# Three unused tiles that shift operands in SBUF by 64 and by 96 bytes

## The chip, the cores and the metric

One core of a Trainium2 chip runs one step of a small diffusion trunk. The metric is the device time of one execution in microseconds. Three runs of the kernel before took 601.01, 600.64 and 601.30 us; the median is 601.01.

## The reference

One layer reads 1024 latent tokens and 128 context tokens of width 1024 (nine tiles of 128 tokens, the last of them context), in float32. Cut to what matters:

```python
mod = silu(cond) @ w_ada + b_ada                 # shift, scale, gate
h = rmsnorm(x, norm_g) * (1 + scale) + shift
u, v, g_a, c_q, c_kv, k_rope, g_b = split(h @ w_in)      # 2496 columns
a_out = chunk_mlp(u, v, w_s, b_s, g_v) * silu(g_a)       # 128x128 position mixing
q = (rmsnorm(c_q, q_norm_g) @ w_uq)                      # 4 heads, 128 + 64 rope
ckv = rmsnorm(c_kv, kv_norm_g); k, val = ckv @ w_ukv
attn = softmax(q k^T / sqrt(192)) @ val   # latent rows see latent and 256 cached keys
y = concat([a_out, attn * silu(g_b)]) @ w_o
out = rmsnorm(x + gate * y, final_g)      # also returned: new_ckv, new_krope
```

## The kernel before, in words

Each float32 operand of a product is split into a high part, rounded to the type that TensorE reads in one pass, and a low part, the remainder. A product is then three matmuls: high by high, high by low, low by high. In `T.matmul(out, a, b)` the operand `a` is the stationary one (loaded 128 columns at a time) and `b` the moving one, whose columns (256, 384, 448 or 512) stream past it. In a row of the profile the moving operand stands first behind the arrow: `o<-ph,vh` moves ph against vh.

The stages follow one another on TensorE:

- head (0 to some 60 us): x and the modulation weights `ada` are loaded (L313, L475), the modulation is computed, x is normalised, transposed and split into `area`, and the v part of the projection starts (L443 to L448, L371 to L373);
- projection (60 to 235 us): the rest of `h @ w_in` on sums of blocks, in runs of matmuls of 384 columns (L928 and L949) that move `area`, the block sums in `w1t`, or the small tiles `t4h` (one) and `t4l` (two), against the weights `w` and `s`;
- q and kv (235 to 310 us): 448-column products (L1371 to L1373), then the parts of q and the keys (L158 to L160);
- attention (310 to 500 us): scores (L1500 to L1504, L1526 to L1533) move the keys `kch`, `kcl`, `krh`, `krl` against q, which lies in `area`; ScalarE writes the exponentials `e` (L1481), GpSimd scales them (L1486), TensorE transposes them (L1609), ScalarE and VectorE split the result into `ph` and `pl`, and the value products (L1633 to L1635) move these against `vh` and `vl`;
- output projection (500 to 592 us): again on block sums, 512-column products (L1970 to L1972) that move parts of `w_o` in `area`, `kch` and its like, `vht`, `vlt`, or in the tail tiles `t` (t4), `t1a`, `t1c`, `t1h`, `t1l`; the stationary blocks are slices of `area` and the rings B and C.

The order of the work on each engine is written by planners in the kernel (`Plan.run`, `merged`, `later`) from costs and due times that stand in the code. None of them looks at an address. TensorE's queue runs in that order, SP issues most loads in program order.

SBUF is handed out from two ends. A pool opened with `side="left"` stands above the left pools opened before it, one with `side="right"` below the right pools opened before it. `ht` (the three `area` tiles) is the first left pool. All later left pools (`w1`, `va`, `vb`, `kv`, `tp`, `wo` and others) stand on top of it, so they move with it. The right pools hold, among others, the identity `ident`, the gates' product `mixB`, the q parts (`cqh`, `wfh`), and, one after the other at the same place, the pool `at` (e, ph, pl) and the pool `ep` of the output stage (tail tiles, gate0, fg, xr, own). Both `at` and `ep` grow from the same lower end upward.

Of the kernel before, what the change touches and what calls it, by code (L numbers as in the profile page):

```python
# [9 lines left out]
F32 = mybir.dt.float32  # L10
# [8 lines left out]
P = 128  # L19
# [75 lines left out]
def tile_hymba_step(ctx: ExitStack, tc: tile.TileContext, I, O):  # L95
# [3 lines left out]
    def opened(name, bufs=1, space=None, side=None):  # L99
        kw = dict(name=name, bufs=bufs, reuse_waits="tile")  # L100
        if space is not None:
            kw["space"] = space
        if side is not None:
            kw["side"] = side
        cm = tc.tile_pool(**kw)
        return cm, cm.__enter__()
# [4 lines left out]
    def lo_of(lo, src, hi):  # L111
        V.tensor_tensor(lo, src, f32(hi), op=ALU.subtract)  # L112
# [54 lines left out]
    def later(dt, fn):  # L167
        waiting.append((now[0] + dt, fn))
        waiting.sort(key=lambda w: w[0])
# [27 lines left out]
    def need(*keys):  # L197

        at_ = now[0]
        while waiting and not made.issuperset(keys):  # L200
            due, fn = waiting.pop(0)
            now[0] = due
            fn()
        now[0] = at_
        assert made.issuperset(keys), keys
# [52 lines left out]


    c_ht, ht = opened("ht", side="left")  # L260
    c_w1, w1 = opened("w1", side="left")
    c_va, va = opened("va", side="left")
    c_vb, vb = opened("vb", side="left")
# [1180 lines left out]
    c_at, ap_ = opened("at", side="right")  # L1444
# [53 lines left out]
    def logits(ps, qs, sl):  # L1498
        qh_, ql_, qr_ = qs
        T.matmul(ps, qh_, kch[:, sl], start=True, stop=False)  # L1500
        T.matmul(ps, qh_, kcl[:, sl], start=False, stop=False)
        T.matmul(ps, ql_, kch[:, sl], start=False, stop=False)
        T.matmul(ps, qr_, krh[:, sl], start=False, stop=False)
        T.matmul(ps, qr_, krl[:, sl], start=False, stop=True)  # L1504
# [229 lines left out]
    def own_steps():  # L1734

        sl, ks = slice(2 * P, 3 * P), slice(NS * P, NT * P)
        four = lambda ap: ap.rearrange("p (h c) -> p h c", h=4)
        cell = {}

        def score():  # L1740
            ps = cell["s"] = pso.tile([P, 512], F32, tag="o", name="s8")
            for h in range(4):
                logits(ps[:, h * P : (h + 1) * P], (qnh[2][:, h, sl], qnl[2][:, h, sl], qr[2][:, 1, h, sl]), ks)
            later(1.3, shift)

        def shift():
            e = cell["e"] = ap_.tile([P, 1280], F32, tag="e", name="e8", bufs=6)
            m = sm.tile([P, 4], F32, tag="m8", name="m8", bufs=1)
            nb = cell["nb"] = sm.tile([P, 4], F32, tag="nb8", name="nb8", bufs=1)
            su = cell["su"] = sm.tile([P, 4], F32, tag="su8", name="su8", bufs=1)  # L1750
            V.tensor_reduce(m, four(cell["s"]), axis=AX.X, op=ALU.max)
            V.tensor_scalar(nb, m, nscl[:, NS : NS + 1], None, op0=ALU.mult)
            for h in range(4):
                c_ = slice(h * P, (h + 1) * P)
                S.activation(e[:, c_], cell["s"][:, c_], AF.Exp, bias=nb[:, h : h + 1], scale=scl[:, NS : NS + 1], accum_out=su[:, h : h + 1])
            later(3.7, divide)

        def divide():
            rs = sm.tile([P, 4], F32, tag="rs8", name="rs8", bufs=1)
            V.reciprocal(rs, cell["su"])  # L1760
            e4 = four(cell["e"][:, :512])
            G.tensor_tensor(e4, e4, rs.unsqueeze(2).broadcast_to([P, 4, P]), op=ALU.mult)
            made.add("e8")

        def tr():
            need("e8")
            ps = pst.tile([P, 512], F32, tag="t", name="pT8")
            for h in range(4):
                T.transpose(ps[:, h * P : (h + 1) * P], cell["e"][:, h * P : (h + 1) * P], ident)
            cell["ph"] = ap_.tile([P, 512], F32R, tag="ph", name="ph8", bufs=4)  # L1770
            cell["pl"] = ap_.tile([P, 512], F32R, tag="pl", name="pl8", bufs=4)
            later(0.5, lambda: S.copy(cell["ph"], ps))

            def low():
                lo_of(cell["pl"], ps, cell["ph"])
                made.add("p8")

            later(1.15, low)

        def av():  # L1780
            need("p8")
            o = cell["o"] = pso.tile([P, 512], F32, tag="o", name="o8")
            T.matmul(o, vh[:, NS, :], cell["ph"], start=True, stop=False)
            T.matmul(o, vh[:, NS, :], cell["pl"], start=False, stop=False)
            T.matmul(o, vl[:, NS, :], cell["ph"], start=False, stop=True)
            cell["os"] = cell["e"][:, 512:1024]

            def out():
                S.copy(cell["os"], o)
                made.add("o8")  # L1790

            later(0.8, out)

        def up():
            need("o8")
            ps = pso.tile([P, 512], F32, tag="o", name="at8")
            for h in range(4):
                T.matmul(ps[:, h * P : (h + 1) * P], wuv[:, h, :], cell["os"][:, h * P : (h + 1) * P], start=True, stop=True)
            d = mixB[:, :, NS * P : NT * P]
            later(1.0, lambda: V.tensor_tensor(d, d, four(ps), op=ALU.mult))  # L1800

        return [(1.1, score), (0.45, tr), (0.65, av), (0.85, up)]

    heads = [(t, h) for t in range(NS) for h in range(4)]
# [267 lines left out]
    def place(name, w, dt=F32R):  # L2072
        return ep.tile([P, w], dt, tag=name, name=name)
# [2 lines left out]
    t1h, t1a = place("t1h", 512), place("t1a", 2048)  # L2076
    gate0, fg = place("gate0", 1024, F32), place("fg", 1024, F32)
    t1c, t1l = place("t1c", 1024), place("t1l", 512)
    t4 += [kv.tile([P, 1024], F32R, tag=n, name=f"{n}t") for n in ("vh", "vl")]
    th[1, 3], tl[1, 3] = t1h, t1l  # L2080
    gate, ssq = {}, {}
# [115 lines left out]
    for q in range(3, len(queue)):  # L2197
        n, name, _ = queue[q]
# [279 lines left out]
```

## Time and profile before

| | before |
|---|---|
| median of three runs | 601.01 us |
| the profiled execution's own time | 600.68 us |
| its span, first to last instruction | 598.9 us |
| mean granted TensorE clock | 0.997 |
| TensorE matmuls, busy | 588.7 us, 3653 |
| weight loads, busy | 527.0 us, 3653 |
| VectorE, ScalarE, GpSimd busy | 428.7, 329.7, 213.5 us |
| DMA | 67.33 MB, mean 112 GB/s |

The weight load of the next matmul runs beside the matmul of now. A matmul's time in a row is the time from its start to the end of its drain, and the next one starts before that, so rows overlap. In the timeline the columns are start (us from the span's start), duration (us, of all merged instructions of the row), engine, line, operation, tiles, shape and count. In the table by stretches they are the stretch, its length, busy us with counts in brackets for TensorE, weight loads, VectorE, ScalarE and GpSimd, the granted clock, the share of the DMA engines and GB/s.

### The profile page before, as it was taken

What the parts mean: (1) busy time and instruction counts of PE and PEld (TensorE: products, weight loads), DVE (VectorE), ACT (ScalarE), POOL (GpSimd) and SP (SyncE); (2) the same over time, 40 slices, a digit from 0 to 9 for tenths busy, and PEclk for the clock granted to TensorE, in tenths of its full rate; (3) what the DMA queues carried; (4) which work ended last, traced back from release to release, by engine and by line L of the source; (5) the groups of instructions that cost most, each with busy time, mean ns of one, the idle gap of its engine ahead of it and who ended that gap; (6) DMA issues with size and microseconds to landing.
All of it is one profiled execution on the core that took longest, in us unless ns stands there. A gap on an engine that the chain in (4) does not pass through costs nothing.

```text
span 598.9 us, 10175 instructions
## 1 busy us (share of the span) xinstructions
PE 588.7 (98%) x3653; PEld 527.0 (88%) x3653; DVE 428.7 (72%) x946; ACT 329.7 (55%) x771; POOL 213.5 (36%) x251
## 2 busy tenths in 40 slices
PE   8999999999999999999999999999999999999995
PEld 7578889999999999999998888888888898888884
DVE  3676888967647467476678677778788876477885
ACT  6665886434323245455567556655756462457543
POOL 2562103200000000343264345454543547269834
PEclk9999999999999999999999999999999999999998
DMA  8991002051050134100002033434242019951444
GB/s 314 366 378 74 1 4 68 1 210 71 7 207 26 45 96 138 42 1 0 2 8 71 0 106 111 156 123 142 85 144 90 1 71 307 359 178 39 140 153 161
DMA packets 31059, 67.33 MB, mean 112 GB/s; under 512 B 3344, under 2 KB 17440, under 8 KB 29984
## 3 DMA queue, kind: packets, MB, share of 16 engines
q1 hardware_dynamic: 27792, 55.93, 26.7%
q0 software_dynamic: 2352, 8.39, 4.1%
q10 hardware_dynamic: 864, 2.36, 1.2%
q8 instruction: 29, 0.48, 0.3%
q14 instruction: 22, 0.18, 0.1%
HBM read 53.45 MB, written 13.21 MB: 111 GB/s over the span
## 4 chain that ended last, share of the span: by engine, by line
PE 92%; DMA 3%; POOL 2%; DVE 1%; ACT 1%; issue 0%; SPq 0%; POOLq 0%; ACTq 0%
PE p L928 15%; PE tp L949 7%; PE pT L1609 5%; PE o L1633 3%; PE o L1635 3%; PE o L1634 3%; PE zacc L1372 2%; PE zacc L1371 2%; PE zacc L1373 2%; PE S L1970 2%; PE S L1971 2%; PE S L1972 2%; DMA ada<-in_ada_ss 2%; PE s L1526 2%; PE s L1529 2%; PE s L1528 2%
## 5 line engine op out<-in xcount | busy, mean ns | idle before, releaser
L1486 POOL TENSOR_SCALAR e<-e,rs 128x1280 f32<-128x1280 f32 x32 | 47.0, 1470 | 96.8 <-DVE rs L1485 64.7
L112 DVE TENSOR_TENSOR pl<-pT,ph 128x512 fp32r<-128x512 f32 x81 | 55.5, 686 | 32.8 <-ACT ph L1613 32.6
L1481 ACT ACTIVATE e<-s,nb,scl 128x256 f32<-128x256 f32 x64 | 56.9, 891 | 38.8 <-DVE nb L1469 26.2
L1613 ACT CAST ph<-pT 128x512 fp32r<-128x512 f32 x80 | 47.2, 590 | 40.6 <-PE pT L1609 40.3
L1219 POOL TENSOR_TENSOR kr<-z,rope 128x64 f32<-128x64 f32 x8 | 2.6, 326 | 154.6 <-ACT z L1228 154.6
L949 PE MATMUL tp<-area,w 128*128 128x384 f32 x288 | 52.5, 337 | 0.0
L1633 PE MATMUL o<-ph,vh 128*128 128x256 f32 x160 | 50.7, 317 | 0.0
L949 PEld LDWEIGHTS tp<-area,w 128*128 128x128 f32 x288 | 50.4, 188 | 0.0
L1609 PE MATMUL pT<-ident,e 128*128 128x128 f32 x320 | 47.9, 272 | 0.0
L1609 PEld LDWEIGHTS pT<-ident,e 128*128 128x128 f32 x320 | 38.9, 140 | 7.2
L1635 PE MATMUL o<-ph,vl 128*128 128x256 f32 x160 | 45.1, 282 | 0.0
L1634 PE MATMUL o<-pl,vh 128*128 128x256 f32 x160 | 44.8, 280 | 0.0
L1463 DVE TENSOR_REDUCE m<-s 128x1 f32<-128x1024 f32 x32 | 38.9, 1216 | 2.6 <-PE s L1504 2.5
L1633 PEld LDWEIGHTS o<-ph,vh 128*128 128x128 f32 x160 | 30.2, 188 | 4.7 <-ACT os L1643 2.9
L1634 PEld LDWEIGHTS o<-pl,vh 128*128 128x128 f32 x160 | 30.3, 189 | 0.4
L1635 PEld LDWEIGHTS o<-ph,vl 128*128 128x128 f32 x160 | 30.1, 188 | 0.0
L928 PE MATMUL p<-area,w 128*128 128x384 f32 x144 | 27.6, 337 | 0.0
L928 PE MATMUL p<-area,s 128*128 128x384 f32 x144 | 27.3, 337 | 0.0
L1371 PE MATMUL zacc<-w1t,area 128*128 128x448 f32 x72 | 27.0, 375 | 0.0
L928 PE MATMUL p<-w1t,s 128*128 128x384 f32 x144 | 26.6, 339 | 0.0
L1372 PE MATMUL zacc<-w1t,area 128*128 128x448 f32 x72 | 26.3, 366 | 0.0
L1373 PE MATMUL zacc<-w1t,area 128*128 128x448 f32 x72 | 26.3, 365 | 0.0
(703 smaller groups left out, 1767.8 us busy)
## 6 DMA issues: line engine op xcount, KB each, us to landing
ada<-in_ada_ss SPq DMA_DIRECT2D x16, 512.0 KB, 8.6
w2r<-in_w_t SPq DMA_DIRECT2D x12, 512.0 KB, 5.3
x<-in_x SPq DMA_DIRECT2D x9, 512.0 KB, 5.6
adag<-in_ada_g SPq DMA_DIRECT2D x4, 1024.0 KB
traw<-in_w_o SPq DMA_DIRECT2D x16, 256.0 KB, 3.0
tdram<-thi SPq DMA_DIRECT2D x32, 128.0 KB, 1.8
tdram<-traw SPq DMA_DIRECT2D x32, 128.0 KB, 1.8
wor<-in_w_o SPq DMA_DIRECT2D x8, 512.0 KB, 3.8
```

Source lines behind the costliest of these rows:

```text
L112: V.tensor_tensor(lo, src, f32(hi), op=ALU.subtract)
L928: T.matmul(banks[key], a_, b_, start=k == 0 and m == 0, stop=k == 3 and m == len(passes) - 1)
L949: T.matmul(tps[c, 2][:, :GW], w_[c][:, k, :], x_[k, 2], start=k == 0 and m == 0, stop=k == NK - 1 and m == 2)
L1371: T.matmul(ps[:, :448], a, wqh[k], start=k == 0, stop=False)
L1463: V.tensor_reduce(m[:, 0:1], lat_, axis=AX.X, op=ALU.max)
L1481: S.activation(e[:, sl], src, AF.Exp, bias=nb, scale=scl[:, t : t + 1], accum_out=su[:, i : i + 1])
L1486: G.tensor_scalar(e, e, rs, 0.0, op0=ALU.mult, op1=ALU.add)
L1609: T.transpose(ps[:, w : w + P], es[t, h][:, c * P : (c + 1) * P], ident)
L1613: later(0.5, lambda: S.copy(ph[:, :w], ps[:, :w]))
L1633: T.matmul(o, vh[:, kt, :], ph[:, sl], start=c == 0, stop=False)
L1634: T.matmul(o, vh[:, kt, :], pl[:, sl], start=False, stop=False)
L1635: T.matmul(o, vl[:, kt, :], ph[:, sl], start=False, stop=c == n - 1)
```

## The change

Three tiles are added that nothing writes or reads. One of 16 float32 (64 bytes in each partition) is the first tile behind `area`'s pool opening, ahead of the `area` tiles, so every left pool stands 64 bytes higher. One of 24 float32 (96 bytes) is asked for in the pool `at` in the first unit of the attention; there `ph` and `pl` keep their places and the `e` tiles lie 96 bytes lower. One of 96 bytes in `ep` does the same for the tail tiles and for gate0 and fg, while `xr` and `own` stay. All instructions, their order on the five queues and what they wait for are the same in the two kernels.

```diff
     c_ht, ht = opened("ht", side="left")
+    ht.tile([P, 16], F32, tag="edge", name="edge2")
     c_w1, w1 = opened("w1", side="left")
     c_va, va = opened("va", side="left")
...
                 T.transpose(ps[:, h * P : (h + 1) * P], cell["e"][:, h * P : (h + 1) * P], ident)
+            ap_.tile([P, 24], F32, tag="edge", name="edge0")
             cell["ph"] = ap_.tile([P, 512], F32R, tag="ph", name="ph8", bufs=4)
...
     t1c, t1l = place("t1c", 1024), place("t1l", 512)
+    place("edge", 24)
```

Where the operands start, as the two built programs place them (bytes past a multiple of 128, before and after):

| tiles | before | after |
|---|---|---|
| area, w1t, kch, kcl, krh, krl, vh, vl, vht, vlt, rings, one t4l | 0 | 64 |
| weights w and s, x, ada, the other t4l (va) | 64 | 0 |
| adag, gv, wsT | 96 | 32 |
| e; t, t1a, t1c, t1h, t1l | 96 | 0 |
| ph, pl, cqh, cql, wfh, wfl, z, xr, own | 96 | 96 |
| ident | 0 | 0 |

Counted by matmul rows of the trace before (each shape with its moving and stationary start, bytes past a multiple of 128):

| columns | rows | before | after | which |
|---|---|---|---|---|
| 512 | 824 | 0, 0 | 64, 64 | v projection, scores, most of the output |
| 384 | 786 | 0, 64 | 64, 0 | projection |
| 256 | 480 | 96, 0 | 96, 64 | value products |
| 128 | 324 | 0, 96 | 0, 0 | transposes of e |
| 448 | 216 | 0, 0 | 64, 64 | q and kv |
| 256 | 207 | 0, 0 | 64, 64 | cached scores, last output tile |
| 512 | 72 | 96, 0 | 0, 64 | output, tail tiles moving |

Both x and ada land 192 bytes past a multiple of 256 before and on a multiple of 256 after.

## The prediction

> **What bounds the kernel now.** I read the engine line of the page first, then the waits of TensorE, then its busy time by stage.
>
> ```profile
> PE 588.7 (98%) x3653; PEld 527.0 (88%) x3653; DVE 428.7 (72%) x946; ACT 329.7 (55%) x771; POOL 213.5 (36%) x251
> ...
> PE warm L454 <- POOL ident masks.py:199: 1.4, 1, 1.4
> PE modp L337 <- DMA ada<-in_ada_ss: 1.1, 3, 0.5
> PE vacc L448 <- DVE area L112: 0.3, 1, 0.3
> ...
> 100.00:235.00 135.00, 135.00 (x829) 132.15 (x829) 93.15 (x195) 53.97 (x111) 3.60 (x3) 1.00 0.24 87
> 310.00:500.00 190.00, 190.00 (x1323) 168.72 (x1322) 144.65 (x308) 114.20 (x248) 90.56 (x91) 1.00 0.28 92
> 525.00:592.00 67.00, 66.92 (x316) 55.69 (x314) 54.86 (x99) 39.47 (x93) 47.72 (x36) 1.00 0.39 130
> ```
>
> The reader is to see that TensorE waits for others 2.8 us in all, and that in the three long stages it is never idle, at granted clock 1.00. A busy matmul overlaps the next one, so the number that sets the time is the step from one start to the next. A change that adds no instruction and no wait can move the time only through that step, or through the few waits at the head. So the views that decide are rows of the timeline, where a step is the difference of two starts.
>
> ```profile
> 127.29 4.40 PE L928 MATMUL p<-w1t,s 128*128 128x384 f32 x24
> 131.53 2.28 PE L928 MATMUL p<-area,s 128*128 128x384 f32 x12
> ...
> 150.44 4.35 PE L928 MATMUL p<-w1t,s 128*128 128x384 f32 x24
> 154.62 0.69 PE L928 MATMUL p<-area,s 128*128 128x384 f32 x3
> ...
> 212.23 4.32 PE L928 MATMUL p<-area,w 128*128 128x384 f32 x24
> 216.39 2.42 PE L928 MATMUL p<-w1t,s 128*128 128x384 f32 x13
> ```
>
> Three runs of 24 products of one shape: (131.53 - 127.29) / 24 = 176.7 ns, (154.62 - 150.44) / 24 = 174.2 ns, (216.39 - 212.23) / 24 = 173.3 ns. The first two read the same two tiles at the same addresses. So the step is not fixed by the addresses alone: a run settles in one of several rhythms and keeps it until something disturbs it. What can disturb it shows here:
>
> ```profile
> 134.88 0.34 PE L928 MATMUL p<-t4l,w 128*128 128x384 f32 x1
> ...
> 135.24 0.34 PE L928 MATMUL p<-t4h,w 128*128 128x384 f32 x1
> 135.41 0.33 PE L928 MATMUL p<-t4l,w 128*128 128x384 f32 x1
> ...
> 209.81 0.33 PE L928 MATMUL p<-t4l,w 128*128 128x384 f32 x1
> ```
>
> The t4l at 134.88 lies 0 bytes past a multiple of 128, like every other moving operand of these runs. The t4l at 135.41 and at 209.81 is the other one, 64 bytes past. Behind the first the rhythm goes from 176.7 to about 174.7, behind the second to the 173.3 of the row at 212.23. A different offset of 64 bytes between two neighbours is thus felt, but it shifts a rhythm and does not stop the stream.
>
> A moving operand at 32 past a multiple of 64 is felt more, at the end of the kernel:
>
> ```profile
> 526.95 0.39 PE L1970 MATMUL A<-area,area 128*128 128x512 f32 x1
> ...
> 529.67 0.39 PE L1970 MATMUL A<-krh,ringB 128*128 128x512 f32 x1
> ...
> 533.81 0.40 PE L1970 MATMUL S<-t1a,area 128*128 128x512 f32 x1
> 534.05 0.40 PE L1971 MATMUL S<-t1a,area 128*128 128x512 f32 x1
> ...
> 536.62 0.39 PE L1970 MATMUL S<-area,ringB 128*128 128x512 f32 x1
> ```
>
> Twelve products from 526.95 to 529.67 take 226.7 ns each, twelve from 533.81 to 536.62 take 234.2. Moving area, kch and the like are at 0 mod 128, t1a, t1c, t1h, t1l and t at 96.
>
> **The change part by part.** No instruction, wait, queue position or buffer is added or moved: the order of all five queues is the same. Only addresses change, so each part is a number of products times a change of step.
>
> *Tail operands, 96 to 0.* 72 products of 512 columns move t or t1*. At the step of the aligned run they save 72 x (234.2 - 226.7) = 0.54 us. Their stationary blocks on the left go from 0 to 64 at once, a pairing that no 512-column row shows; the 384-column rows with that pairing (moving 0, stationary 64) are the runs above and reach 173.3, so I take the gain, and keep 0 as the other end. The products right behind such a run (532.43 vht to 533.59) are slow too though they lie at 0, and recover. Four such exits cost some 25 ns each, 0.1 us more. Together **-0.6 us**, from -0.6 to 0.
>
> *Value products.* 480 products of 256 columns move ph and pl, which stay at 96, against vh and vl, which go from 0 to 64.
>
> ```profile
> 430.94 0.28 PE L1635 MATMUL o<-ph,vl 128*128 128x256 f32 x1
> 431.06 0.28 PE L1633 MATMUL o<-ph,vh 128*128 128x256 f32 x1
> 431.18 0.28 PE L1634 MATMUL o<-pl,vh 128*128 128x256 f32 x1
> 431.29 0.28 PE L1635 MATMUL o<-ph,vl 128*128 128x256 f32 x1
> 431.41 0.40 PE L1526 MATMUL s<-kch,area 128*128 128x512 f32 x1
> 431.65 0.39 PE L1527 MATMUL s<-kcl,area 128*128 128x512 f32 x1
> 431.87 0.39 PE L1528 MATMUL s<-kch,area 128*128 128x512 f32 x1
> 432.10 0.39 PE L1529 MATMUL s<-krh,area 128*128 128x512 f32 x1
> 432.33 0.60 PE L1609 MATMUL pT<-ident,e 128*128 128x128 f32 x4
> ...
> 173.63 0.28 PE L1042 MATMUL gps<-hig,selr 128*2 128x256 f32 x1
> 173.75 0.28 PE L1042 MATMUL gps<-log,selr 128*2 128x256 f32 x1
> ...
> 588.88 0.28 PE L1999 MATMUL left<-area 128*128 128x256 f32 x1
> ...
> 590.33 0.28 PE L1999 MATMUL left<-area,area 128*128 128x256 f32 x1
> ```
>
> Their step is (431.41 - 430.94) / 4 = 117.5 ns. The gps products pair 96 with 64 at the same width: 116 to 118 ns over their four pairs, 120 ns here. The other 256-column rhythm is that of left, (590.33 - 588.88) / 12 = 120.8. A step of 116.7 would save 480 x 0.8 = 0.4 us; one of 120 would cost 1.2, one of 115 would save 1.2. I take **-0.4**, since gps is the nearest pairing, with -1.2 and +1.2 as ends.
>
> *Score products.* Some 250 products of 512 columns follow value products or transposes four or five at a time. The four from 431.41 to 432.33 take 0.92 us, 230 ns each, against the settled 226.7: 250 x 3.3 = 0.8 us are lost in settling. Both operands move by 64, but what stands ahead moves otherwise, so they start at another point. I take **-0.3**; ends -0.8 and +1.0 (all at 231 to 234).
>
> *Runs of 384 columns.* 786 products, both operands on the left, both moved. Their mean step is near 175: between the ends 173.3 and 176.7 lie -1.3 and +1.3 us. The rhythms are drawn anew at each entry, so **0**.
>
> *Transposes of e, and the engines on e.*
>
> ```profile
> L1486 POOL TENSOR_SCALAR e<-e,rs 128x1280 f32<-128x1280 f32 x32 | 47.0, 1470 | 96.8 <-DVE rs L1485 64.7
> L1609 PE MATMUL pT<-ident,e 128*128 128x128 f32 x320 | 47.9, 272 | 0.0
> ...
> L365 PE MATMUL h<-ident,x 128*128 128x128 f32 x24 | 3.9, 272 | 0.0
> ```
>
> Transposes with a stationary block at 96 (e) and at 64 (x) both last 272 ns, so its offset doesn't show. GpSimd waits 96.8 us ahead of its 32 e rows, and TensorE waits for none of them. **0**; a GpSimd twice as slow on e (1.5 us more a row) would cost at most the 1.5 us of the last row, since that wait covers the others.
>
> *The head.* TensorE's first real work waits for loads:
>
> ```profile
> 2.12 5.58 DMA x<-in_x
> 7.71 11.42 DMA ada<-in_ada_ss
> ```
>
> x and ada land 192 bytes past a multiple of 256 before, at 0 after. **0**, at most -0.5 (3% of 17.0). The Trainium skill, in "DMA: Bandwidth & Descriptors", section "How a descriptor splits into AXI transactions", says that a transfer which does not start on a 256-byte boundary pays beats for the bytes ahead of it; no run here has such a destination aligned. By its count a 4 KB row from 192 takes 134 beats and one from 0 takes 128, which as an estimate would be -0.8 us on these 17.0.
>
> Sum: -0.6 - 0.4 - 0.3 = **-1.3 us**. The profiled execution took 600.68 us (its span 598.9 and 1.8 around it), so 599.4; the median of the runs is 601.01, 0.33 above, so **599.7** is what I expect to be timed, 0.2% faster.
>
> **The rivals.** *Nothing that counts.* The tail alone aligns, the rest keeps its rhythms: -0.6, or 0 if even that depends on the place in memory and not on the offset (all tail tiles at 96 also lie high in memory, so the rows do not part the two). 600.4 to 601.0. For it: nine tenths of the matmul time has both operands moved alike. The Trainium skill's "SBUF — State Buffer", section "Specifications (TRN2)", gives lines of 16 bytes; every offset here is a multiple of 32 before and after, so by that rule nothing would change. The t1a rows against the area rows speak against it.
>
> *Slower: the left side loses its good offset.* If a moving stream is at its best only at 0 mod 128, and 64 acts like the 96 of t1a, all 512-column products on the left, 824 of them with a mean step of 229.0, go towards 234.2: up to 824 x 5.2 = +4.3 us, less the 0.6 of the tail: 604.7. It decides from an added 2.2 ns a product (1.8 us, against the 0.6 saved). For it: 227 is reached in the quoted rows only at 0. Against it: the t4l rows at 64 show no longer step at 384 columns (0.33 against 0.34 in length, and a faster rhythm behind two of them).
>
> *A faster head,* by the 256-byte boundary: 600.2 to 600.5 alone, more with the forecast's other terms.
>
> **How the numbers follow.** The forecast has 0.46, nothing that counts 0.30, the slower left side 0.17, the head as main effect 0.07. A measurement of this kernel tells about 0.2% from no change, 1.2 us: faster is under 599.8, slower over 602.2. The forecast's own range is 598.4 to 600.6, of its 0.46 some 0.40 is faster and 0.06 within; the second case gives 0.29 within and 0.01 slower; the third 0.17 slower; the head, with the tail beside it, 0.05 faster and 0.02 within. So faster 0.45, same 0.37, slower 0.18. The range reaches below to where the runs of 384 and the value products both fall well (-1.3 - 1.2 - 0.6 - 0.8 = -3.9, at 597.1) and above to half the price of the slower left side: 597.0 to 603.0.
>
> **What would show it.** In the profile after: the twelve S<-t1a products from first start to the next tile in 2.72 us and not 2.81, and vht behind t at 227; o products at 116 to 117 ns a step; runs of 24 L928 products still at 173.3, 174.7 or 176.7 and no fourth value; x and ada rows of the chain within 0.3 us of 17.0. L1970 products with moving area at over 229 would be the slower rival. I am wrong if the 384-column or 512-column runs on the left take up a step that stands nowhere above.

## The result

| | before | after |
|---|---|---|
| median | 601.13 us (13 runs, 600.46 to 601.49) | 602.02 us (13 runs, 601.67 to 602.80) |
| ratio | | 1.0016, 95% interval 1.0009 to 1.0023 |
| the profiled execution's own time, its span | 600.68, 598.9 us | 602.79, 601.0 us |
| mean granted TensorE clock | 0.997 | 0.996 |

The kernel became 0.89 us slower. This is inside the 0.2% that the prediction called no change, and inside its range, but the sign of the forecast was wrong. The profiled execution of after lies 0.77 us above its median; it has a late load at the head, shown below, that is no part of the result.

The engine line on the page of after:

```profile
PE 590.4 (98%) x3653; PEld 527.6 (88%) x3653; DVE 431.4 (72%) x946; ACT 329.3 (55%) x771; POOL 212.4 (35%) x251
```

and the waits of TensorE in it (us in total, times, longest):

```profile
PE warm L455 <- POOL ident masks.py:199: 1.4, 1, 1.4
PE vacc L449 <- DVE area L112: 1.0, 2, 0.6
PE modp L338 <- DMA ada<-in_ada_ss: 0.8, 2, 0.5
PE xT L366 <- DVE x L406: 0.2, 1, 0.2
```

The same instructions, the same few waits at the head, and behind them no wait of a matmul. Weight loads, which have an engine row of their own (PEld), also wait for others, nearly the same in both kernels (for `os` 3.1 us each, for instance), but one is new in after, in the output stage:

```profile
558.24 0.19 PEld L1974 LDWEIGHTS S<-t1a,ringC 128*128 128x128 f32 x1 [0.30 <-DVE ringC L112]
```

VectorE is late with `ringC` there, because one of its rows takes 4.45 us where it took 1.71 before:

```profile
550.05 4.45 DVE L2180 SCALAR_TENSOR_TENSOR xr<-xr,fss,fg 128x1024 f32<-128x1024 f32 x1
```

Two products of that place take 257 and 343 ns, so the wait costs some 0.14 us. It does not follow from the addresses: of the runs below, kick has it with the addresses of before, and kicka does not have it with those of after. Apart from it the time sits in the steps of the matmuls again. (Lines of after are 1 to 3 higher: L1653 is the L1652 of before, L1972 its L1970.) Four products mark off the stages: the `at` products of the context tile, a w product at the end of the attention, the first `A` and the last `left`. In the timeline of before:

```profile
325.62 1.05 PE L1798 MATMUL at<-e,wuv 128*128 128x128 f32 x8
...
500.05 0.39 PE L2000 MATMUL w<-area,area 128*128 128x512 f32 x1
...
525.56 0.39 PE L1970 MATMUL A<-area 128*128 128x512 f32 x1
...
591.64 0.28 PE L2001 MATMUL left<-area,ml 128*128 128x256 f32 x1
```

and of after:

```profile
326.75 1.06 PE L1800 MATMUL at<-e,wuv 128*128 128x128 f32 x8
...
502.12 0.40 PE L2002 MATMUL w<-area,area 128*128 128x512 f32 x1
...
527.55 0.40 PE L1972 MATMUL A<-area 128*128 128x512 f32 x1
...
593.75 0.28 PE L2003 MATMUL left<-area,ml 128*128 128x256 f32 x1
```

The attention took 500.05 - 325.62 = 174.43 us and takes 502.12 - 326.75 = 175.37: **+0.94**. The output stage took 66.08 and takes 66.20: +0.12, where the tail was to save 0.6; the wait for `ringC` alone makes up the 0.12, and without it the stage would be about as long as before. Between them -0.08. Worked out in the same way from starts, the q and kv stage (235 to 310 us) costs +0.20, and 60 to 235 us +0.02.

Inside the attention the unit that repeats is one pair of heads of one latent tile; it ends with an `at<-os` row. These rows of before, some of twelve:

```profile
352.98 0.61 PE L1652 MATMUL at<-os,wuv 128*128 128x128 f32 x4
364.86 0.60 PE L1652 MATMUL at<-os,wuv 128*128 128x128 f32 x4
376.73 0.60 PE L1652 MATMUL at<-os,wuv 128*128 128x128 f32 x4
...
459.80 0.60 PE L1652 MATMUL at<-os,wuv 128*128 128x128 f32 x4
```

and of after:

```profile
354.15 0.61 PE L1653 MATMUL at<-os,wuv 128*128 128x128 f32 x4
366.10 0.61 PE L1653 MATMUL at<-os,wuv 128*128 128x128 f32 x4
378.05 0.61 PE L1653 MATMUL at<-os,wuv 128*128 128x128 f32 x4
...
449.73 0.61 PE L1653 MATMUL at<-os,wuv 128*128 128x128 f32 x4
```

Before, seven pairs from 376.73 to 459.80 take 11.867 us each; after, eight from 354.15 to 449.73 take 11.947. By the undivided starts every pair repeats its length to 1 ns: in before 11.907, 11.880 and then nine times 11.866 or 11.867, in after eleven times 11.946 or 11.947. The attention is thus not many products that settle one way or the other; the whole pair runs in a **cycle of a fixed length**, and after runs in one that is 80 ns longer. The eleven pairs make 0.83 of the 0.94 us, since two of before's are still longer. Split by products over the stage, the 48 even groups of four score products cost 0.57 us more, the value products 0.31, the other score products 0.06, the transposes -0.05.

### The profile page after: what moved, and what is told of

Its sections match the earlier page's. It is cut to its first block, busy times and chain, and to the rows that moved or that the text cites. A ratio compares the mean times of both kernels' runs of the same rounds, so it can differ in the third digit from the quotient of the medians.

```text
span 601.0 us, 10175 instructions
## 1 busy us (share of the span) xinstructions
PE 590.4 (98%) x3653; PEld 527.6 (88%) x3653; DVE 431.4 (72%) x946; ACT 329.3 (55%) x771; POOL 212.4 (35%) x251
## 4 chain that ended last, share of the span: by engine, by line
PE 94%; DVE 2%; DMA 2%; ACT 1%; SPq 1%; POOL 1%; issue 0%; POOLq 0%; ACTq 0%
PE p L929 15%; PE tp L950 7%; PE pT L1610 6%; PE o L1634 4%; PE o L1635 3%; PE o L1636 3%; PE zacc L1374 2%; PE zacc L1372 2%; PE zacc L1373 2%; PE S L1974 2%; PE S L1972 2%; PE S L1973 2%; PE s L1527 2%; PE s L1530 2%; PE s L1528 2%; PE s L1529 2%
```

## The experiments

"Trace from 60 us" in the tables below is the difference to before, in one profiled execution each, from the first product past 60 us to the end of the span; so it leaves the loads at the head out. In after, tail96, ep96, right224, left224 and tail224w it holds the wait for `ringC`, 0.11 to 0.15 us, as their last stage does; the trace of before has no such wait. Its output stage starts at the two products ahead of the first `A`. The starts are given past a multiple of 512; everything on the left that TensorE reads (area, keys, vh, vl, rings, vht, vlt) shares one start, "left". Theories are lettered anew for each round of runs, as the expectations say.

### Left or right side, alone and together

Four kernels: the change without its right-hand tiles (left64), without its left tile (right96), the left tile together with all right pools but that of the identity moved by the same 64 bytes (both64), and a left tile of 32 bytes alone (left32). Theory R: a step follows from how operands lie to each other and from what ran ahead. Rival A: the start itself counts. Rival N: the loads of the head differ from run to run.

left64 against before (left32 has 8 in place of 16):

```diff
     c_ht, ht = opened("ht", side="left")
+    ht.tile([P, 16], F32, tag="edge", name="edge2")
```

right96 against before:

```diff
+            ap_.tile([P, 24], F32, tag="edge", name="edge0")
             cell["ph"] = ap_.tile([P, 512], F32R, tag="ph", name="ph8", bufs=4)
...
     t1c, t1l = place("t1c", 1024), place("t1l", 512)
+    place("edge", 24)
```

both64 against left64:

```diff
     c_pc, pc = opened("pc", side="right")
+    pc.tile([P, 16], F32, tag="edge", name="edge3")
```

> Only the tile of 64 bytes on the left; e and the tail tiles stay at 96. Theory R (a step depends on how the moving and the stationary operand lie to each other and on what ran ahead; moving both alike changes nothing): the 786 rows of 384 columns keep their steps one by one (138.6 us); the value and score products change as in the changed kernel, some +0.9 us between 310 and 500 us; the tail products keep 233 to 234 or lose a little; in all 0.7 to 1.5 us slower than before. Rival A (the absolute start of the moving operand counts): every product on the left changes its step, the last 512-column products by as much as the score products. Rival N (the 0.9 us is spread of the loads at the head): same time as before within 0.3 us, attention within 0.2 us.

> Only the two tiles of 96 bytes on the right; the left side stays. Theory R: attention within 0.2 us of before, since e is only a stationary operand of transposes; the 72 tail products go from 233.6 to the 226.7 ns of aligned products and those behind them recover at once: -0.6 us; in all -0.6 us against before. If the tail products stay at 230 or more, their place in memory and not their start counts. Rival N: as before within 0.3 us.

> The left side 64 bytes up and all right pools but the first (identity, constants, w_uv) 64 bytes down, which is the same modulo 128: e, ph, pl, the q parts and the tail tiles start at 32 instead of 96, so every pair of left and right operands lies to each other as before, modulo 128. Theory R with period 128 or less: attention and tail as before within 0.2 us, in all as before. If the period is longer than 128 bytes: attention changes by some +-1 us. Rival A: as the changed kernel or slower.

> A tile of 32 bytes on the left instead of 64: nearly all operands of products start 32 bytes past a multiple of 64. Theory R: the 384-column rows keep their steps (138.6 us) though they now start off 64, the last 512-column products with both operands on the left keep 226.7 ns, only the products that pair left and right change, within +-1.5 us in all. Rival A, lines of 64 bytes or more: one line more for each moving operand, 512-column products from 226.7 to 233, all of them together 3 us or more slower.

| | left | e | tail | median, ratio (interval) | trace from 60 us | attention | q, kv | 525 to the last product | pair of heads, us |
|---|---|---|---|---|---|---|---|---|---|
| before | 128 | 352 | 352 | 601.09 | 0 | 0 | 0 | 0 | 11.867 |
| after | 192 | 256 | 256 | 602.02 (before 601.13), 1.0016 (1.0009 to 1.0023) | +1.22 | +0.94 | +0.20 | +0.10 | 11.947 |
| left64 | 192 | 352 | 352 | 601.23, 1.0007 (0.9998 to 1.0015) | +0.61 | +0.34 | +0.25 | +0.02 | 11.893 |
| right96 | 128 | 256 | 256 | 601.88, 1.0013 (1.0005 to 1.0022) | +0.52 | +0.81 | 0.00 | -0.15 | 11.905, 11.949, 11.953 |
| both64 | 192 | 288 | 288 | 602.54, 1.0028 (1.0018 to 1.0039) | +1.62 | +1.24 | +0.27 | +0.15 | 11.967 |
| left32 | 160 | 352 | 352 | 601.73, 1.0012 (1.0003 to 1.0021) | +0.71 | +0.70 | +0.10 | -0.05 | 11.940 |

Every one is slower than before in the attention, each with its own cycle; in right96 three lengths take turns. R missed twice in right96: it expected the attention within 0.2 us of before and the tail at 226.7 ns, and they came to +0.81 us and 232.4 ns. The parts don't add: 0.34 and 0.81 give 0.94. Rival A falls in the projection: its 792 products of 384 columns take a mean step (nine steps over 250 ns left out) of 175.07, 175.08, 175.08, 175.07, 175.07 and 175.10 ns in these six, though both operands start at three different places. Moving two operands alike changes nothing there; the 3 us that A priced for left32 are absent too. In the attention both64 moves nearly everything alike, the identity not, and is the slowest of all, so R's first half (moved alike, nothing changes) held only where no other operand comes in between. Rival N is dealt with under the head, below.

### e and the tail, parted

e96 and tail96 each have one of right96's two lines; e32 is e96 with 8 in place of 24. ep96 has the tile behind ph and pl, so that these move too:

```diff
             cell["pl"] = ap_.tile([P, 512], F32R, tag="pl", name="pl8", bufs=4)
+            ap_.tile([P, 24], F32, tag="edge", name="edge0")
```

> Only the e tiles move, from 96 to 0 past a multiple of 128; up to 500 us every address is that of the kernel with both right-hand tiles. Theory R (the step is a rhythm fixed by the addresses of the operands and of what ran ahead, the same in each execution): the attention (326 to 500 us) is slower than before by the 0.81 us measured with both right-hand tiles, within 0.05, the four-group scores at 231.7 ns, and the output stage (525 to 592) is as before within 0.1; median 601.9. Rival C (the rhythm falls anew in each execution): the attention differs from before by some other number, between -1 and +1 us. Rival N (the moved e tiles cost nothing, the difference lay in the loads): 601.1, attention within 0.1 of before.

> Only the tail tiles and gate0, fg move, from 96 to 0. Theory R: all of the kernel up to 525 us is as before, group by group within 0.1 us of before's 173.99 in the attention, and the output stage gains 0.1 to 0.15 as with both right-hand tiles; median 601.0. The prediction's term: tail products at 226.7 instead of 233.6 ns, -0.6 us, median 600.5. Rival C: the attention differs from before by more than 0.2 us with no address changed there.

> e, ph and pl all move from 96 to 0 (the pool grows from below them), vh and vl stay at 0; beside the kernel with e alone moved this is the step of ph and pl. The prediction's reading of the value products (a pair with another start is better or worse by up to 2.5 ns of 117.9): now the pair is 0 with 0, as in the 256-column rows left<-area at 120.8, so +1.4 us on 480 products beside e alone, 603.3. Theory R: no rule from the pair's starts, the value products stay within 0.5 ns of 117.9 and the attention within 0.6 us of that with e alone moved, either way.

> e moves from 96 to 64, by 32 bytes. If the start past a multiple of 64 decides for e (0 and 64 alike, 32 and 96 alike), the attention is slower than before by 0.8 us as with e at 0, 601.9. Theory R: another rhythm again, attention anywhere from -0.8 to +0.8 of before, four-group scores between 226.7 and 234 ns; the transposes themselves stay at 30.45 us within 0.05. Rival N: 601.1.

| | e | ph, pl | tail | median (before 601.03), ratio | trace from 60 us | attention | value product, ns | four-group score, ns | pair of heads, us |
|---|---|---|---|---|---|---|---|---|---|
| before | 352 | 352 | 352 | | 0 | 0 | 117.9 | 229.6 | 11.867 |
| e96 | 256 | 352 | 352 | 601.76, 1.0014 (1.0005 to 1.0023) | +0.71 | +0.81 | 118.3 | 231.7 | 11.905, 11.949, 11.953 |
| e32 | 320 | 352 | 352 | 601.42, 1.0008 (1.0000 to 1.0017) | +0.35 | +0.51 | 118.3 | 231.3 | 11.913 |
| ep96 | 256 | 256 | 352 | 601.96, 1.0016 (1.0007 to 1.0025) | +1.03 | +1.02 | 118.8 | 231.9 | 11.953 |
| tail96 | 352 | 352 | 256 | 602.13, 1.0017 (1.0008 to 1.0026) | +1.04 | 0.00 | 117.8 | 229.6 | 11.867 |

Two things follow for the attention. It is the same in each execution of the same addresses: e96 repeats right96's +0.81 and its three lengths, tail96 repeats before's time to 0.01 us. Rival C falls. And e alone is enough, although it is only the stationary operand of transposes whose own 320 steps don't grow (30.49 us in all before, 30.45 in e96). What changes is the step of the products behind them. Nine score products behind the first transposes of e, with the next start behind them, in before:

```profile
319.98 0.39 PE L1501 MATMUL s<-kcl,area 128*128 128x512 f32 x1
...
322.05 0.40 PE L1783 MATMUL o<-ph,vh 128*128 128x512 f32 x1
```

and in e96, at the same addresses of these products themselves:

```profile
320.64 0.39 PE L1501 MATMUL s<-kcl,area 128*128 128x512 f32 x1
...
322.68 0.40 PE L1784 MATMUL o<-ph,vh 128*128 128x512 f32 x1
```

2.07 / 9 = 230.0 ns against 2.04 / 9 = 226.7. Here the moved e is the better one, at once settled; over the pairs the cycle that begins so is the longer one. So a good entry is no sign of a good cycle. The value products give no rule either: with e at 256, ph and pl alike with vh past a multiple of 128 (ep96: 256 and 128) they come to 118.8, not to the 120.8 that the rows of `left` would say, and not within R's 0.5 ns of 117.9. e32 answers that 64 is no period for e: 320 lies as far past a multiple of 64 as 256, and has another cycle.

tail96 has another surprise: 1.09 us in the stretch from 500 to 525 us, where no matmul operand moved. Among its waits stands:

```profile
PE S L1971 <- DMA t1l<-tdram: 1.0, 1, 1.0
```

GpSimd's queue in its timeline, with the idle time ahead and what ended it:

```profile
512.16 0.59 POOL L1966 DMA_DIRECT2D t1a<-tdram  x1 [3.75 <-DVE area L112]
...
514.65 0.53 POOL L2121 DMA_DIRECT2D t1l<-tdram  x1 [0.28 <-PE o L1635]
```

and in that of before:

```profile
508.32 0.59 POOL L1966 DMA_DIRECT2D t1a<-tdram  x1
...
514.52 0.53 POOL L2120 DMA_DIRECT2D t1l<-tdram  x1 [1.68 <-PE o L1635]
```

The DMA view of tail96 and then of before (us from issue to landing last):

```profile
t1l<-tdram POOLq DMA_DIRECT2D x1, 256.0 KB, 11.6
```

```profile
t1l<-tdram POOLq DMA_DIRECT2D x1, 256.0 KB, 7.7
```

In before, t1a begins exactly where the buffer of the last raw piece of w_o (`wor7`, one of the six of e) ends. Moved down alone, its first 96 bytes lie in that buffer, so its load waits for the last reader of wor7, 3.84 us longer; t1c, t1h and t1l share its queue, t1l is issued when it was before but lands 3.9 us later, with the others now crowded ahead of it in the queue, and TensorE waits 1.0 us. In after and right96 e's buffers move down with the tail, so they don't overlap. This is a cost of a move by bytes that none of the theories had.

### The tail at the start of all others

In the tail the moved tiles start 0 past a multiple of 128 like everything on the left, and still step at 232.4 ns (right96), not at 226.7. Past a multiple of 512, though, they are at 256 and the left side at 128. So the next two make the starts equal by that measure, from either side.

right224 is right96 with 56 in place of 24 in both lines (224 bytes); left224 is left64 with 56 in place of 16.

> The two right-hand tiles hold 224 bytes in place of 96, nothing else moves: e and the tail tiles start 128 bytes past a multiple of 512, as every matmul operand on the left does (before: 352, with 96 bytes: 256). Theory G (what counts is whether moving and stationary operand, and the neighbours in the stream, start alike past a multiple of 512, not past one of 128): the tail products fall from 233.6 to 226.7 ns and the vht and vlt behind them from 230 to 231 to 226.7, output stage (525 to 592) -0.6 to -0.8 us. Theory R without a rule: tail at 230 to 234 ns again, output within 0.2 of before. For the attention G says only that it changes; by R and by what e at 0 and at 64 gave (+0.81 and +0.51), -0.5 to +1.0 us. Median 600.0 to 601.6 by G, 601.0 to 602.1 by R.

> One unused tile of 224 bytes at the start of the left side, none on the right: all left operands start 352 bytes past a multiple of 512, where e, ph, pl and the tail tiles lie and stay. Theory G: tail products and those behind them at 226.7 ns, output -0.6 to -0.8 us; the projection (both operands move) within 0.1 us of before; the value products, now 352 with 352, at the 119.8 ns of the 256-column rows whose operands are both on the left, +0.9 us, or at 113 to 114 (half of 226.7), -2.0; the score products change, -0.8 to +1.0. Median 599 to 602. Theory R without a rule: tail at 230 to 234 ns, o anywhere from 116.6 to 119.2, median 601.0 to 602.5.

Medians 601.21 (1.0002, 0.9993 to 1.0011) and 602.13 (1.0019, 1.0010 to 1.0028), before 601.05. Twelve tail products and the next start, in right224:

```profile
534.44 0.39 PE L1971 MATMUL S<-t1a,area 128*128 128x512 f32 x1
...
537.16 0.39 PE L1971 MATMUL S<-area,ringB 128*128 128x512 f32 x1
```

and the same twelve in after:

```profile
535.82 0.40 PE L1972 MATMUL S<-t1a,area 128*128 128x512 f32 x1
...
538.58 0.40 PE L1972 MATMUL S<-area,ringB 128*128 128x512 f32 x1
```

2.72 us, 226.7 ns each, against 2.76, 230.0 (before 2.81). In left224 it is 226.7 too, with all of them at 352. The products behind the tail are clean as well, and the output stage gains 0.43 and 0.46 us. Both have the wait for `ringC`, which takes 0.15 and 0.11 us of it; without it they would gain 0.58 and 0.57. Theory G holds here: in a long stream of products of 512 columns the step is the shortest when all operands start alike past a multiple of 512 (a multiple of 256 would say the same of these kernels; 128 would not). It is not shown for other widths: the projection's runs of 384 columns reach their shortest step, 173.3 ns, with the moving operand at 128 and the stationary one at 192. In the attention G does not hold: it took +0.70 (pairs of 11.941 and 11.913 in turn) and +1.11 (11.960), with the value products of left224, 352 with 352, at 118.8 ns and not at G's 119.8 or 113; the q and kv stage of left224 took +0.43.

### The tail alone, without its overlap; and all alike in the attention

tail224w against before:

```diff
-            r = ap_.tile([P, 1280], F32, tag="e", name=f"wor{k}", bufs=6)[:, :1024]
+            r = ap_.tile([P, 1024], F32, tag="e", name=f"wor{k}", bufs=6)
...
     t1c, t1l = place("t1c", 1024), place("t1l", 512)
+    place("edge", 56)
```

all352 is left224 with the identity taken from the right pool to the left one, behind the unused tile:

```diff
-    ident = pc.tile([P, P], F32, tag="ident", name="ident")
+    c_ht, ht = opened("ht", side="left")
+    ht.tile([P, 56], F32, tag="edge", name="edge2")
+    ident = ht.tile([P, P], F32, tag="ident", name="ident")
```

> The tail tiles alone at 128 past a multiple of 512 (224 bytes lower), e stays at 352; the last three raw pieces of w_o are asked for as tiles of 1024 columns instead of the first 1024 of 1280, so that the moved t1a does not lie over the end of one of them and its load keeps its time. Theory G with R: attention as before within 0.05 us (no address changed there), t1a issued at 508.3 as before and not at 512.2, tail products and those behind them at 226.7 ns, output -0.43 us; median 600.5, about 0.1% under before. If the wait of the tail moved by 96 bytes alone was not for that overlap, t1l is late again by 1 us, 601.5.

> One unused tile of 224 bytes at the start of the left side, and the identity moved from the right to the left side, so that identity, e, ph, pl, q parts, tail tiles and everything on the left start 352 past a multiple of 512; beside left224 this moves the identity alone. Theory G applied to the attention: with no pair and no neighbour unlike, the four-group scores go from 229.6 to 226.7 ns (-0.56 us), the five-group ones from 230.2 and 118.1 to 226.7 and 119.8 (-0.3, +0.3), the value products from 117.9 to 119.8 to 120 (+0.9 to +1.0), output -0.46; attention +0.4, median 601.0. Theory R without a rule for the attention: four-group scores at 229 to 234 and value products at 116.6 to 119.2 again, attention +0.3 to +1.2, median 601 to 602.

tail224w: **600.61 us** (600.07 to 602.32, 11 runs; before 601.22), ratio 0.9993, interval 0.9984 to 1.0002. Its attention is before's to 0.01 us, t1a is issued without a wait, and the output stage gains 0.45:

```profile
525.85 0.39 PE L1970 MATMUL A<-area 128*128 128x512 f32 x1
...
534.01 0.39 PE L1970 MATMUL S<-t1a,area 128*128 128x512 f32 x1
...
536.73 0.39 PE L1970 MATMUL S<-area,ringB 128*128 128x512 f32 x1
...
591.49 0.28 PE L2001 MATMUL left<-area,ml 128*128 128x256 f32 x1
```

It is the one kernel here whose median and trace both lie under before's; the trace says by 0.54 us (it has the wait for `ringC` too, 0.15 us), while the interval of the timed ratio reaches 1. So the gain is shown in the trace and not by the timing.

all352: 602.36 us (1.0017, 1.0009 to 1.0026). Output -0.62, but attention +1.14, four-group scores at 231.9 ns, value products at 118.7, pairs of 11.960. The wait for `ringC` is absent here, so 0.62 is the whole gain of equal starts in the output stage. G fails in the attention: with identity, e, ph, pl, q, keys and values all at 352 the groups of four and five are still entered from transposes of 128 columns, and the pair has a long cycle. One operand of the pair is not alike even so: w_uv, the stationary one of the four `at` products that end it, stays at 480. But four-group scores with only operands at 352 around them still take 926 to 929 ns, against 4 x 226.7 = 907. With the identity at 384 (left224) or at 352 the pair settles at the same 11.960 us.

### What picks the cycle

Was it the addresses, or only the state in which the stream came into the attention? Three products said twice, of 512, 256 and 128 columns, disturb it at unchanged addresses, in before (kick), e96 (kicke) and after (kicka).

```diff
+            if t == 2 and h0 == 0 and x == 0 and c.start == 0:
+                T.matmul(ps, a, kch[:, c], start=True, stop=True)
             T.matmul(ps, a, kch[:, c], start=x == 0, stop=False)
...
+                if t == 3 and pr == 1 and c == 0:
+                    T.matmul(o, vh[:, kt, :], ph[:, sl], start=True, stop=True)
...
+                    if t == 5 and pr == 0 and c == 0 and w == 0:
+                        T.transpose(ps[:, w : w + P], es[t, h][:, c * P : (c + 1) * P], ident)
```

> The kernel before with three products said twice: one score product of 512 columns at the first head pair of latent tile 2, one value product of 256 columns in tile 3, one transpose of e of 128 columns in tile 5; each writes again what the next one writes. No address changes. In the traces so far one pair of heads takes 11.910, 11.875 and from then on 11.867 us in the kernel before, each time. Theory A (the addresses decide, the repeating stream is drawn to one cycle): after each of the three disturbances the pair comes back to 11.867 within three pairs. Theory I (the entry decides, and several cycles live side by side at the same addresses): after at least one of them it stays at another length, 11.87 to 11.97, up to the next disturbance. Time +0.23, +0.12 and +0.11 us for the products themselves and, by A, under 0.3 us more.

> The same three repeated products in the kernel with e alone moved by 96 bytes, whose pairs go round in three lengths, 11.909, 11.947 and 11.951 us. Theory A: back to this round of three after each disturbance, none of it at 11.867. Theory I: at least one of them leaves it in another cycle, 11.867 among the possible ones.

> The same three repeated products in the changed kernel, whose pairs take 11.947 us each. Theory A: back to 11.947 after each disturbance. Theory I: another length stays after at least one.

One execution each (602.12, 602.56 and 602.53 us); only their traces are used. The `at<-os` rows of kick around the first disturbance:

```profile
341.64 0.61 PE L1658 MATMUL at<-os,wuv 128*128 128x128 f32 x4
353.78 0.61 PE L1658 MATMUL at<-os,wuv 128*128 128x128 f32 x4
365.66 0.60 PE L1658 MATMUL at<-os,wuv 128*128 128x128 f32 x4
377.53 0.60 PE L1658 MATMUL at<-os,wuv 128*128 128x128 f32 x4
389.40 0.60 PE L1658 MATMUL at<-os,wuv 128*128 128x128 f32 x4
```

The lengths of all pairs, worked out from the starts (the disturbed ones in brackets):

```
before                11.907 11.880 11.866 11.867 11.867 11.866 11.867 11.866 11.867 11.867 11.866
kick                 [12.141] 11.879 11.867 11.867 11.866 [11.986] 11.934 11.873 [12.006] 11.934 11.874
after                 11.946 11.947 11.947 11.946 11.947 11.947 11.946 11.947 11.947 11.946 11.947
kicka                [12.180] 11.947 11.946 11.947 11.947 [12.066] 11.947 11.947 [12.053] 11.947 11.946
e96                   11.905 11.950 11.952 11.905 11.949 11.953 11.905 11.949 11.952 11.905 11.949
kicke                [12.193] 11.905 11.949 11.952 11.905 [12.070] 11.899 11.946 [12.040] 11.905 11.949
```

Theory A holds as far as the pairs reach: after falls back to 11.947 in the very next pair, e96 into its round of three at another phase (to 6 ns behind the second disturbance), before to 11.867 two pairs behind the first and to 11.873 and 11.874 two pairs behind the second and third, where the next disturbance or the end cuts the return short. In this loop the addresses pick the cycle; for these three disturbances the entry only sets how long it takes to reach it.

## Why the prediction was wrong

**Transposes of e, 0: the step that failed.** "Transposes with a stationary block at 96 (e) and at 64 (x) both last 272 ns, so its offset doesn't show" read the length of the transposes alone. Their steps indeed stay. But e's start decides in which state the next products begin, and e96 alone costs 0.81 us in the trace, 0.73 in the medians. The left tile alone costs 0.34 there and both together 0.94, so how much of the 0.94 is e's can't be parted.

**Score products, -0.3: wrong in sign.** "What stands ahead moves otherwise, so they start at another point" was right; that another point would be the better one was taken from nothing but the room above the settled 226.7. The 48 groups of four give +0.57, the other score products +0.06. Both this and the next term were priced as if each entry were drawn by itself. A pair of heads repeats, so one cycle holds for all of them.

**Value products, -0.4:** +0.30 (117.9 to 118.3 ns), inside the stated ends of 1.2 on either side. The gps rows were no model for it. The mean steps (the 412 of the 480 that are under 150 ns) by the starts of ph and pl and of vh and vl are 117.9 (352 and 128), 116.6 (352 and 160, left32), 118.0 and 118.3 (352 and 192, left64 and after), 118.8 (352 and 352, left224; 256 and 128, ep96) and 119.2 (288 and 192, both64); and 117.9 turns to 118.3 when e alone moves.

**Tail operands, -0.6:** right in size, wrong in the measure of the start. The quoted rows show the left at 128 past a multiple of 512 and the tail at 352; the prediction reduced this to 0 and 96 past 128. With equal starts past 512 the tail does take 226.7 ns and the stage gains 0.43 to 0.46 beside the wait for `ringC`, 0.62 without it: the 0.6 was there, but not at 96 to 0. The change gives 256 against 192, and 230.8 ns in place of 233.6: -0.20 on 72 products, of which that wait takes 0.14 and the products of the same stage with a moving operand on the left 0.13 back (227.6 to 228.2 ns). The doubt that stood among the rivals, that the rows didn't part the offset from the place in memory, is settled: it is the offset, since left224 leaves the tail where it was.

**448-column products: a term that was missing.** The table of rows has 216 of them, the sum doesn't. They go from 202.7 to 203.7 ns (the 206 steps under 250 ns), +0.2, and to 203.2 to 204.4 in every kernel that moves the left side. In both64 they step as before up to 241 us; behind the first transposes and fold products among them they take up another cycle.

**Runs of 384 columns, 0:** right in the number, with no fourth rhythm: 139.67 and 139.68 us for 792 products. The reason given, rhythms drawn anew at each entry, is not what the traces show: of 791 steps between 60 and 235 us, 788 are those of before to 1 ns, so each run takes the rhythm that it took. Nor do the quoted t4l rows show what an offset of 64 does. Both t4l tiles stand in both places, the one at 134.88 and 209.27, the other at 135.41 and 209.81, and behind the two places the rhythms still differ, 174.8 and 173.3 ns:

```profile
209.27 0.34 PE L928 MATMUL p<-t4l,w 128*128 128x384 f32 x1
209.45 0.34 PE L928 MATMUL p<-w1t,w 128*128 128x384 f32 x1
209.63 0.34 PE L928 MATMUL p<-t4h,w 128*128 128x384 f32 x1
209.81 0.33 PE L928 MATMUL p<-t4l,w 128*128 128x384 f32 x1
```

**The head, 0:** right in the trace of after, and open beyond it. Up to 20 us the three kernels with x and ada on a 256-byte boundary need +0.08 (after), -0.69 (left64) and +0.01 us (both64), the ten others -0.27 to +0.32; the -0.69 is more than the 0.5 that the prediction allowed, and the 3% behind that bound came from no row. The chain of after shows why its profiled execution is long:

```profile
4.52 9.15 DMA x<-in_x
...
16.75 0.48 DVE area L112
...
25.00 0.73 PE vacc L449 x2
```

x lands at 13.67 us, VectorE's work on it is late, and the vacc product at 25.00 waits 0.59 us for an area row. left64 has the same left side and no such wait (its 20 to 30 us take +0.02, those of after +0.90, of both64 +0.86). So rival N was right for this one execution: the trace from 60 us on says +1.22, the medians +0.89. A hint of a faster head remains: in eight of the ten kernels with x and ada off the boundary, the difference of the medians agrees with the trace from 60 us to 0.10 us (in right96 and all352 it is 0.27 and 0.31 above), in the three on it the medians are 0.33, 0.47 and 0.17 lower (of the 0.33, after's, the wait for `ringC` can be 0.14). The Trainium skill's "DMA: Bandwidth & Descriptors", section "How a descriptor splits into AXI transactions", by which the prediction estimated -0.8, is neither borne out by these traces nor refuted by the medians; with one trace each and medians that vary by some tenths this stays open.

**The rivals.** *The left side loses its good offset* had the right sign by luck: the cost did not come from an offset that is bad for every stream. A settled stream of products with everything on the left at 192 runs in after as it did at 128:

```profile
555.26 0.39 PE L1973 MATMUL S<-area,ringB 128*128 128x512 f32 x1
...
557.30 0.39 PE L1973 MATMUL S<-area,ringB 128*128 128x512 f32 x1
```

nine products in 2.04 us, 226.7 ns. *Nothing that counts* priced the whole at 600.4 to 601.0, and the sign of the attention makes it miss by a microsecond. Its "nine tenths of the matmul time has both operands moved alike" was too high as well: 427.8 us of the 590 do, seven tenths. The 16-byte lines of the Trainium skill's "SBUF — State Buffer", section "Specifications (TRN2)", as the prediction read them, would let moves by 32 bytes change nothing. Here 32 bytes on e alone make each pair of heads 11.913 in place of 11.867 us, and 32 on the left 11.940. *A faster head* is the hint above. The range, 597.0 to 603.0, held the 602.02, but that is no merit of the sum: its terms for e, the scores and the value products had the wrong size or sign, and only the smallness of every effect kept the time inside.

Open is why a given set of starts has the cycle that it has. No rule in the starts was found for the attention; ten other layouts of the attention's tiles gave nine other cycles or rounds of cycles, all longer than that of before; the two kernels that leave these tiles in place kept it.

## What to carry to other kernels

Where TensorE never waits, a move by a few bytes still changes the step of products, and in a loop it does so through a cycle that the whole body falls into: read the length of the repeating body over several turns, not the mean of a kind of product, and expect no sum of parts. In a long stream of 512-column products give all operands one start past a multiple of 512; in a body that mixes widths and transposes, try layouts and measure. Look at the waits of the weight loads as well as at those of the matmuls; here one of them hid a quarter of the tail's gain. Before moving a tile inside a reused pool, look which buffers it will then lie over: 96 bytes of overlap cost more than the alignment brought.

## What the runs showed that was not expected

The steps of TensorE in the attention repeat to the nanosecond between executions: before, tail96 and tail224w, three kernels with the same addresses up to the output stage, have the same 174.43 us of attention, right96 and e96 the same 175.24. This is not so everywhere: in the projection of tail96, at the addresses of before, one run of twelve 384-column products takes 173.3 ns in place of 176.7 and the stretch is 0.11 us shorter. A disturbance of 0.1 to 0.3 us in the attention is forgotten within one or two pairs, or to 7 ns where the next one comes first. The start of a *stationary* operand in 128-column transposes (e) shows in the products behind them (230.0 to 226.7 ns at once, 0.81 us more in the end) and not in the transposes. And products of 256 columns go below their even step: 119.8 ns where `left` has all operands alike, 116.6 in the value products of left32, whose operands are unlike, while those of 512 columns are at their shortest, 226.7, when all are alike.
